# Two-layer encoder trunk: three PSUM accumulators for turned products and one for dense products, with pauses between dense blocks

## The chip, the core and the metric

The kernel runs on one core of a Trainium2 chip. The metric is the device time of one execution in microseconds. All computation is in float32 formats; products are made from pairs of a rounded part and its remainder.

## The reference

The input is a sequence of 2048 frames of width 1024. Layer 0 is a pooling mixer, layer 1 is attention; both end in a gated embedding add. Cut to what matters:

```python
# layer 0: h = rms_norm(x); u, z = split(h @ w_in); trailing means of u, group maps, * silu(z), @ w_out
# keys and values once from the stream after layer 0 (16 heads of 64)
def stick_breaking_attention(q, k, v):          # A[t,s] = beta[t,s] * prod_{s<j<t} (1 - beta[t,j])
    for blk in range(S // 128):
        logits = einsum('bhtd,bhsd->bhts', q_blk, k[:L]) * d ** -0.5
        log_keep = where(s < t, log_sigmoid(-logits), 0)
        later = cumsum(log_keep, reverse) - log_keep
        a = where(s < t, exp(log_sigmoid(logits) + later), 0)
        out = a @ v[:L]
# layer 1: x = x + (attention * silu(z)) @ b_w_out
# both layers: x = x + (p[i] @ ple_w[i]) * sigmoid(x @ ple_gate_w[i])
```

## The kernel before

The frames are cut into four chunks of 512. The first part (lines 144 to 547) runs layer 0, the keys and values and the queries for all chunks. It has PSUM pools of its own and is not touched.

The second part (from line 550) is attention with the rest of layer 1 beside it. PSUM has eight banks of 128x512 float32, and the pools divide them: `psl` (2) for logits, `psa` (2) for turned (transposed) products, `pso` (2) for a head's output, `psd` (2) for the dense products of the rest of the layer.

Chunks of queries are taken from the last (3) to the first (0). For each there are 16 heads, and for each head the chunks of keys from the queries' own down to 0: these are the slots. A slot has four steps `n`, one for 128 queries each. So chunk 3 has 256 steps, chunk 2 has 192, chunk 1 has 128 and chunk 0 has 64. The loop at line 808 issues in each step:

- `front` (lines 603 to 611): two matmuls into a `psl` tile (on the diagonal narrower ones and a third for the mask), a sigmoid on ScalarE into one of four `kap` tiles, and on VectorE a scan that makes running products into a `pp` tile.
- `turn` (lines 622 to 626), for the slot's step six steps back: up to four 128x128 transposes into a `psa` tile, a copy of it to `at[:, 0]` on ScalarE, and on VectorE the subtraction that makes the remainder `at[:, 1]`. The `psa` tile is free after both.
- some pieces of the `filler` (see below).
- `gather` (lines 634 and 635), for the step eight back: two matmuls of `at[:, 0]` and `at[:, 1]` with the values into the head's `pso` tile. After a head's last step ScalarE and VectorE take the output (lines 639 and 640), and after two heads GpSimd multiplies it by the gate (line 647).

The filler is a Python generator for dense work that has no part in the recurrence. Beside chunk 3 it is `gate_z`: the gate z for all four chunks, 32 blocks of 24 matmuls (lines 663, 665, 667), each read by VectorE (`zr`, line 704). Beside chunk 2 it is `post(3)`: the output projection, 8 blocks of 24 read by VectorE (`xr`, line 728); then for each of 8 column blocks the gate's 24 matmuls, read by ScalarE (`sg`, line 750), and 6 matmuls of the embedding, read by VectorE (line 753), and four transposes of the result into a `psa` tile (`psao`, line 760). The embedding itself is turned into `psa` tiles too (`psap`, line 737). Beside chunk 1 runs `post(2)`, beside chunk 0 `post(1)`. `post(0)` runs alone at the end, the tail, and takes three of four accumulators from `psl` and the fourth from `psd`.

`piecewise` yields after each matmul, and the loop draws as many pieces in a step as the rate says: pieces in all by steps of the chunk (`POSTZ / 64.0` is 3 a step, `POST / (64.0 * c3 - 2 * LAG_G)` is 2.5, 3.9 and 9.2). What it does not draw in a step is owed to the next.

The order in which the loop issues is a priority: a scheduler then places the instructions of each engine, with its own reckoning of when operands and buffers are there. Each engine runs its instructions in the placed order.

Of the kernel before, what the change touches and what calls it, by code (L numbers as in the profile page):

```python
# [8 lines left out]
F32 = mybir.dt.float32  # L9
# [5 lines left out]
P = 128  # L15
# [6 lines left out]
W5 = 512  # L22
# [8 lines left out]
def f(ap):  # L31
    return ap.bitcast(F32)
# [3 lines left out]
def trunk_kernel(ctx, tc, x, p, a_norm, a_w_in, a_w_group, a_scale, a_w_out, kv_norm, w_kv,  # L36
# [103 lines left out]
    def pair(nm):  # L140
        return act.tile([P, 2, W5], F32R, tag="act", name=nm)


    with ExitStack() as st:
# [4 lines left out]
        psd = st.enter_context(tc.tile_pool(name="psd", bufs=6, space=bass.MemoryType.PSUM))  # L149
        pst = st.enter_context(tc.tile_pool(name="pst", bufs=2, space=bass.MemoryType.PSUM))  # L150

        def dense():
            return psd.tile([P, W5], F32, tag="psd", name="psd")
# [396 lines left out]
    with ExitStack() as st:  # L550
# [1 line left out]
        t2 = st.enter_context(tc.tile_pool(name="s2", bufs=2))  # L552
        kap = st.enter_context(tc.tile_pool(name="kap", bufs=1))
        psl = st.enter_context(tc.tile_pool(name="psl", bufs=2, space=bass.MemoryType.PSUM))
        psa = st.enter_context(tc.tile_pool(name="psa", bufs=2, space=bass.MemoryType.PSUM))
        pso = st.enter_context(tc.tile_pool(name="pso", bufs=2, space=bass.MemoryType.PSUM))
        psd = st.enter_context(tc.tile_pool(name="psd2", bufs=2, space=bass.MemoryType.PSUM))

        NK = 4
        kaps = [kap.tile([P, W5], F32, name=f"kap{i}") for i in range(NK)]  # L560
# [89 lines left out]
        tail = [0]  # L650

        def dense():
            if tail[0] and tail[0] % 4:
                tail[0] += 1
                return psl.tile([P, W5], F32, tag="psl", name="psdt")
            if tail[0]:
                tail[0] += 1
            return psd.tile([P, W5], F32, tag="psd", name="psd")

        def piecewise(ps, units, acts, c0):  # L660
# [9 lines left out]
        def stored(src):  # L670
            units = []
            for u in [src[:, 0], src[:, 1]] if len(src.shape) == 5 else [src]:
                pr = wpair.tile([P, 2, u.shape[2], P], F32R, tag="wpair", name="wpair")
                nc.sync.dma_start(out=f(pr), in_=u)
                units.append(pr)
            return units

        def pair_up(c):

            if len(ogs[c]) < len(outs[c]):  # L680
                os = outs[c][len(ogs[c])]
                pr = pair("og")
                A.copy(out=pr[:, 0], in_=os)
                V.tensor_tensor(out=pr[:, 1], in0=os, in1=f(pr[:, 0]), op=ALU.subtract)
                ogs[c].append(pr)

        def gate_z(c):

            xs = chunk[c]["x2"] if c == NSUB - 1 else []
            for o in range(len(xs), KT):  # L690
                pr = pair("xz")
                nc.sync.dma_start(out=f(pr), in_=x2p[c][o])
                xs.append(pr)
            ps = psa.tile([P, 4, P], F32, tag="psa", name="psar")
            for j in range(4):
                T.transpose(ps[:, j, :], r2s[c][:, j : j + 1].to_broadcast([P, P]), ident)
            rb = t2.tile([P, W5], F32, tag="rb", name="rb", bufs=1)
            A.copy(out=rb, in_=ps.rearrange("q j t -> q (j t)"))
            for o in range(KT):
                wz = stored(wzd[o])  # L700
                ps = dense()
                yield from piecewise(ps, wz, xs, 0)
                zr = t2.tile([P, W5], F32, tag="tmp", name="zr", bufs=4)
                V.tensor_tensor(out=zr, in0=ps, in1=rb, op=ALU.mult)
                sg = t2.tile([P, W5], F32, tag="tmp", name="sgz", bufs=4)
                A.activation(out=sg, in_=zr, func=AF.Sigmoid)  # L706
                G.tensor_tensor(out=zr, in0=zr, in1=sg, op=ALU.mult)  # L707
                nc.sync.dma_start(out=zd[c][o], in_=zr)
                if c == 0:
                    pair_up(NSUB - 1)  # L710

        POSTZ = 8 * 24
        POST = 8 * 24 + 8 * 30 + 9

        def post(c):

            pin = t2.tile([P, 4, PLE], F32, tag="pin", name="pin", bufs=1)
            nc.sync.dma_start(out=pin, in_=p[1, 0, c * W5 : (c + 1) * W5, :].rearrange("(j q) n -> q j n", q=P))
            x3, og = [], ogs[c]
            while len(og) < 8:  # L720
                pair_up(c)
            for o in range(KT):
                wo = stored(wod[o])
                xr = t2.tile([P, W5], F32, tag="tmp", name="xr", bufs=4)
                nc.sync.dma_start(out=xr, in_=x2d[c][o])
                ps = dense()
                yield from piecewise(ps, wo, og, 0)
                V.tensor_tensor(out=xr, in0=ps, in1=xr, op=ALU.add)
                pr = pair("x3")
                A.copy(out=pr[:, 0], in_=xr)  # L730
                G.tensor_tensor(out=pr[:, 1], in0=xr, in1=f(pr[:, 0]), op=ALU.subtract)
                x3.append(pr)
            pt_ = []
            for k in range(2):
                pt = psa.tile([P, W5], F32, tag="psa", name="psap")
                for j in range(4):
                    T.transpose(pt[:, j * P : (j + 1) * P], pin[:, j, k * P : (k + 1) * P], ident)
                pr = t2.tile([P, 2, W5], F32R, tag="ple", name="ple")
                A.copy(out=pr[:, 0], in_=pt)
                V.tensor_tensor(out=pr[:, 1], in0=pt, in1=f(pr[:, 0]), op=ALU.subtract)  # L740
                pt_.append(pr)
            yield
            late = []
            for o in range(KT):
                wg = stored(wgd[o])
                wl = stored(wld[o])
                ps = dense()
                yield from piecewise(ps, wg, x3, 0)
                sg = t2.tile([P, W5], F32, tag="tmp", name="sg", bufs=4)
                A.activation(out=sg, in_=ps, func=AF.Sigmoid)  # L750
                pl = dense()
                yield from piecewise(pl, wl, pt_, 0)
                V.tensor_tensor(out=sg, in0=pl, in1=sg, op=ALU.mult)
                (V if tail[0] else G).tensor_tensor(out=sg, in0=sg, in1=f(x3[o][:, 1]), op=ALU.add)
                V.tensor_tensor(out=sg, in0=sg, in1=f(x3[o][:, 0]), op=ALU.add)

                def finish(o=o, sg=sg):
                    pt = psa.tile([P, 4, P], F32, tag="psa", name="psao")
                    for j in range(4):
                        T.transpose(pt[:, j, :], sg[:, j * P : (j + 1) * P], ident)  # L760
                    ot = t2.tile([P, 4, P], F32, tag="ot", name="ot", bufs=1)
                    A.copy(out=ot, in_=pt)  # L762
                    nc.sync.dma_start(
                        out=out[0, c * W5 : (c + 1) * W5, o * P : (o + 1) * P].rearrange("(t q) n -> q t n", q=P),
                        in_=ot)

                if late:
                    late.pop()()
                late.append(finish)
                if c:  # L770
                    pair_up(c - 1)
                yield
            late.pop()()
            yield

# [15 lines left out]
        active, filler, owed, head = {}, beside(NSUB - 1), 0.0, {}  # L791
        rate = POSTZ / 64.0
        LAG_T, LAG_G = 6, 8
# [14 lines left out]
        for n in range(4 * len(slots) + LAG_G):  # L808
            i, j = divmod(n, 4)
            if i < len(slots):  # L810
                c, h, kc = slots[i]
                if j == 0:
                    if i == 0:
                        begin(0)
                    if i + 1 < len(slots):
                        begin(i + 1)
                front(active[i], j)
            i2, j2 = divmod(n - LAG_T, 4)
            if 0 <= i2 < len(slots):
                turn(active[i2], j2)  # L820
            owed += rate
            while owed >= 1.0:
                next(filler, None)
                owed -= 1.0
            i3, j3 = divmod(n - LAG_G, 4)
            if 0 <= i3 < len(slots):
                gather(active[i3], j3)
                if j3 == 3:
                    st3 = active.pop(i3)
                    c3 = st3["c"]  # L830
                    if len(outs[c3]) == 8 and c3 not in done:
                        done.add(c3)
                        for _ in filler:
                            pass
                        if c3:
                            filler = beside(c3 - 1)
                            rate = POST / (64.0 * c3 - 2 * LAG_G)
                            owed = 0.0
# [31 lines left out]
```

## Time and profile before

| | us |
|---|---|
| median of 3 runs | 2885.43 (2884.45 to 2885.85) |
| profiled execution | 2880.44 |
| its span, first to last instruction | 2878.4 |
| start of attention | 1422.3 |
| start of the tail | 2777 |

The profile gives busy time of each engine, groups of instructions by line, and who waited for whom. PE is TensorE's matmul side and PEld its weight loads; a wait of PEld begins when the load could have begun, so it is longer than the same wait on PE. DVE is VectorE, ACT ScalarE, POOL GpSimd. Matmuls overlap in the trace: a row's length is from start to drained, and their pace is seen from the starts of neighbours. Some matmul records are missing. L626 is line 626 of the kernel before.

### The profile page before, as it was taken

Reading aid. Unit: us, or ns where it says so; the run is one execution under the profiler, and the core shown is the slowest. Engines: PE = TensorE matmul, PEld = TensorE weight load, DVE = VectorE, ACT = ScalarE, POOL = GpSimd, SP = SyncE. Lnnn points to the kernel's source line nnn. Section 1 sums busy time; section 2 is a strip of 40 time slices with the busy share of each in tenths; the row PEclk is TensorE's granted clock in tenths of the full one; section 3 lists DMA queues with packets and bytes.
Section 4 is the critical chain, followed back from the end, with each engine's and each line's share of the span. In section 5 each row is a group of like instructions: output and inputs, shape, how many; then the busy total and the mean of one; then the engine's idle time right before and its main releaser. Section 6 shows DMA issues by size and latency. Waiting matters only on the chain. (4 is left out here: it accounts for less than half of the span.)

```text
span 2878.4 us, 40091 instructions
## 1 busy us (share of the span) xinstructions
PE 2784.2 (97%) x13923; PEld 2297.6 (80%) x13923; DVE 1910.2 (66%) x2584; ACT 1407.0 (49%) x2765; POOL 856.8 (30%) x710
## 2 busy tenths in 40 slices
PE   8899999999999999999999999999999999999999
PEld 6688887888878888888777888787878778878877
DVE  6555534455455544455299999999999998886642
ACT  5444523345334542345355555556666665554431
POOL 3564346542574326643211111110100011111110
PEclk9899999999999999999999999999999999999999
DMA  7855697456954578346756565455555565567764
GB/s 271 279 185 200 208 299 236 142 191 220 317 199 164 196 229 299 103 153 209 219 182 222 164 213 168 157 164 178 165 158 164 161 189 183 186 189 250 233 205 159
DMA packets 335134, 576.39 MB, mean 200 GB/s; under 512 B 32783, under 2 KB 161839, under 8 KB 334933
## 3 DMA queue, kind: packets, MB, share of 16 engines
q1 hardware_dynamic: 329032, 565.39, 60.0%
q10 hardware_dynamic: 5900, 8.46, 1.0%
q8 instruction: 110, 1.80, 0.3%
q14 instruction: 92, 0.75, 0.1%
HBM read 433.16 MB, written 132.19 MB: 196 GB/s over the span
## 5 line engine op out<-in xcount | busy, mean ns | idle before, releaser
L362 PE MATMUL psd<-wpair,x 128*128 128x512 f32 x2304 | 543.9, 393 | 0.0
L609 ACT ACTIVATE kap<-psl 128x512 f32<-128x512 f32 (+3 forms) x640 | 341.8, 534 | 410.7 <-PE psl L604 258.8
L611 DVE TENSOR_TENSOR_SCAN pp<-kap,pp,zeros 128x512 f32<-128x512 f32 x384 | 513.7, 1339 | 30.0 <-ACT kap L609 28.2
L362 PEld LDWEIGHTS psd<-wpair,x 128*128 128x128 f32 x2304 | 428.1, 188 | 86.2
L626 DVE TENSOR_TENSOR at<-psa,at 128x512 fp32r<-128x512 f32 (+3 forms) x640 | 373.8, 585 | 16.7 <-ACT at L625 15.7
L622 PE MATMUL psa<-ident,pp 128*128 128x128 f32 x2176 | 350.6, 276 | 32.8 <-DVE at L626 30.1
L625 ACT CAST at<-psa 128x512 fp32r<-128x512 f32 (+3 forms) x640 | 331.3, 518 | 38.4 <-PE psa L622 34.5
L622 PEld LDWEIGHTS psa<-ident,pp 128*128 128x128 f32 x2176 | 251.4, 141 | 111.6 <-DVE at L626 68.3
L611 DVE TENSOR_TENSOR_SCAN pp<-kap,zeros 128x128 f32<-128x128 f32 (+3 forms) x256 | 228.8, 895 | 69.6 <-ACT kap L609 67.8
L603 PE MATMUL psl<-kk,qa 128*128 128x512 f32 (+3 forms) x640 | 234.3, 366 | 5.8 <-ACT vr L399 5.8
L634 PE MATMUL pso<-at,vv 128*128 128x512 f32 (+3 forms) x640 | 235.2, 368 | 0.7 <-ACT at L625 0.6
L604 PE MATMUL psl<-kk,qb 128*128 128x512 f32 (+3 forms) x640 | 234.3, 366 | 0.0
L635 PE MATMUL pso<-at,vv 128*128 128x512 f32 (+3 forms) x640 | 233.4, 365 | 0.0
L133 PE MATMUL psd<-xp,wpair 128*128 128x512 f32 x512 | 200.9, 393 | 7.9 <-ACT wpair L116 5.4
L117 DVE SCALAR_TENSOR_TENSOR wpair<-wraw,gains,wpair 128x512 fp32r<-128x512 f32 x192 | 149.9, 787 | 87.7 <-ACT wpair L116 87.4
L116 ACT ACTIVATE wpair<-wraw,gains 128x512 fp32r<-128x512 f32 x192 | 137.4, 720 | 137.5 <-DMA wraw<-in_w_kv_dram 85.6
L135 PE MATMUL psd<-xp,wpair 128*128 128x512 f32 x512 | 200.0, 391 | 2.6 <-DVE wpair L117 2.6
L134 PE MATMUL psd<-xp,wpair 128*128 128x512 f32 x512 | 200.2, 391 | 0.0
L707 POOL TENSOR_TENSOR zr<-zr,sgz 128x512 f32<-128x512 f32 x32 | 62.9, 1964 | 444.6 <-ACT sgz L706 296.2
L112 POOL TENSOR_TENSOR wpair<-wraw,wpair 128x512 fp32r<-128x512 f32 x107 | 145.7, 1366 | 80.3 <-ACT wpair L110 57.4
L110 ACT CAST wpair<-wraw 128x512 fp32r<-128x512 f32 x160 | 96.7, 618 | 121.8 <-PE psd L135 71.0
L603 PEld LDWEIGHTS psl<-kk,qa 128*128 128x128 f32 x640 | 120.7, 189 | 26.5 <-ACT vr L399 6.2
(209 smaller groups left out, 5594.1 us busy)
## 6 DMA issues: line engine op xcount, KB each, us to landing
wpair<-wi SPq DMA_DIRECT2D x96, 512.0 KB
kk<-kd SPq DMA_DIRECT2D x320, 128.0 KB
vv<-vd SPq DMA_DIRECT2D x160, 256.0 KB
wraw<-in_w_kv_dram SPq DMA_DIRECT2D x128, 256.0 KB
wpair<-wzd SPq DMA_DIRECT2D x64, 512.0 KB
wpair<-wod SPq DMA_DIRECT2D x64, 512.0 KB
wpair<-wgd SPq DMA_DIRECT2D x64, 512.0 KB
wi<-wpair SPq DMA_DIRECT2D x32, 512.0 KB
```

The source lines that it names most:

```text
L133: T.matmul(ps, wst(units, kt, 0, c0), acts[kt][:, 0], start=(kt == order[0]), stop=False)
L134: T.matmul(ps, wst(units, kt, 0, c0), acts[kt][:, 1], start=False, stop=False)
L362: T.matmul(pss2[i], ck["x2"][kt][:, xh, tk], wst(ws, kt, wh, 0, W5), start=(kt == 0 and xh == 0 and wh == 0), stop=(kt == KT - 1 and wh == 1))
L603: T.matmul(ps[:, :w], qa[:, qs], kk[:, :w], start=True, stop=False)
L604: T.matmul(ps[:, :w], qb[:, qs], kk[:, :w], start=False, stop=not st["diag"])
L609: A.activation(out=kp[:, r0:], in_=ps[:, :w], func=AF.Sigmoid, scale=-1.0)
L611: V.tensor_tensor_scan(out=pp[:, r0:][:, ::-1], data0=kp[:, r0:][:, ::-1], data1=zeros.to_broadcast([P, w]), initial=1.0 if st["diag"] els ...
L622: T.transpose(pt[:, j * P : (j + 1) * P], pp[:, r0 + kt * P : r0 + (kt + 1) * P], ident)
L625: A.copy(out=at[:, 0, cs], in_=pt[:, cs])
L626: V.tensor_tensor(out=at[:, 1, cs], in0=pt[:, cs], in1=f(at[:, 0, cs]), op=ALU.subtract)
L634: T.matmul(po[:, cs], vv[:, kt, :], at[:, 0, cs], start=(st["diag"] and kt == 0), stop=False)
L635: T.matmul(po[:, cs], vv[:, kt, :], at[:, 1, cs], start=False, stop=(st["last"] and kt == 3))
```

## The change

`psa` gets a third bank and `psd` keeps one. The filler now yields a marker, `PAUSE`, after each dense block, and the loop stops drawing pieces for the rest of the step when it meets one; what is owed stays owed. In the embedding add there is one between the gate's block and the embedding's as well. The rates count the markers (3.1 a step in chunk 3, 2.6, 4.1 and 9.5 after). In the tail the accumulators come in turn from `psl`, `pso` and, one in five, `psd`.

In the placed order of the changed program nothing differs before attention. At its start 24 dense matmuls stand ahead of the third front instead of 36. In chunk 3 the dense matmuls keep their places but for one block end of each head, where the two gather matmuls go ahead of the next block. In chunks 2 to 0 the next block begins a `front`, a `turn` and a `gather` after the end of the one before, where it often followed at once; the steps that lose their dense matmuls so are followed by fuller ones. A dozen of the readers move ahead of a scan on VectorE, some move behind one. No instruction is added.

```diff
-        psa = st.enter_context(tc.tile_pool(name="psa", bufs=2, space=bass.MemoryType.PSUM))
+        psa = st.enter_context(tc.tile_pool(name="psa", bufs=3, space=bass.MemoryType.PSUM))
...
-        psd = st.enter_context(tc.tile_pool(name="psd2", bufs=2, space=bass.MemoryType.PSUM))
+        psd = st.enter_context(tc.tile_pool(name="psd2", bufs=1, space=bass.MemoryType.PSUM))
...
         def dense():
-            if tail[0] and tail[0] % 4:
-                tail[0] += 1
-                return psl.tile([P, W5], F32, tag="psl", name="psdt")
+
             if tail[0]:
                 tail[0] += 1
+                if tail[0] % 5:
+                    pool, tag = ((psl, "psl"), (pso, "pso"))[tail[0] % 2]
+                    return pool.tile([P, W5], F32, tag=tag, name="psdt")
             return psd.tile([P, W5], F32, tag="psd", name="psd")
...
                 if c == 0:
                     pair_up(NSUB - 1)
-
-        POSTZ = 8 * 24
-        POST = 8 * 24 + 8 * 30 + 9
+                yield PAUSE
+
+        PAUSE = "the one accumulator is being read"
+        POSTZ = 8 * 25
+        POST = 8 * 25 + 8 * 32 + 2
...
                 x3.append(pr)
+                yield PAUSE
...
                 A.activation(out=sg, in_=ps, func=AF.Sigmoid)
+                yield PAUSE
                 pl = dense()
...
                 if c:
                     pair_up(c - 1)
-                yield
+                yield PAUSE
...
             owed += rate
             while owed >= 1.0:
-                next(filler, None)
                 owed -= 1.0
+                if next(filler, None) == PAUSE:
+                    break
```

## The prediction

> **What bounds the kernel now.** I read the page's busy shares first, then the attention part cut into stretches, one for each chunk of queries (3, 2, 1, 0) and the tail, and then who TensorE waits for in each.
>
> ```profile
> PE 2784.2 (97%) x13923; PEld 2297.6 (80%) x13923; DVE 1910.2 (66%) x2584; ACT 1407.0 (49%) x2765; POOL 856.8 (30%) x710
> ...
> 1422.30:1949.10 526.80, 509.29 (x2769) 420.71 (x2770) 474.00 (x561) 297.32 (x594) 78.58 (x40) 0.99 0.58 184
> 1949.10:2315.20 366.10, 352.27 (x1982) 289.86 (x1980) 344.74 (x432) 227.66 (x467) 36.29 (x25) 1.00 0.54 166
> 2315.20:2585.20 270.00, 262.26 (x1484) 219.58 (x1482) 236.68 (x308) 156.60 (x340) 33.44 (x24) 1.00 0.60 186
> 2585.20:2777.00 191.80, 184.43 (x1031) 156.45 (x1030) 121.63 (x191) 94.16 (x225) 32.20 (x25) 1.00 0.71 227
> 2777.00:2878.40 101.40, 95.09 (x439) 78.48 (x437) 23.52 (x34) 15.43 (x26) 10.31 (x8) 0.98 0.56 182
> ```
>
> The columns behind the length are PE, weight loads, VectorE, ScalarE, GpSimd, clock and DMA. TensorE is busy 96 to 97% of each attention stretch, but VectorE is close behind in the first two: 474.00 of 526.80 (90%) and 344.74 of 366.10 (94%). In the third it is 88% and in the fourth 63%. So chunk 3 is TensorE's by a little, chunk 2 belongs to both, chunks 1 and 0 are TensorE's. The clock was 0.99 or 1.00, so it has no part in this. Nothing ahead of 1422 us is touched.
>
> What TensorE waits for in attention is one thing, the accumulator of turned products. The rows give time in all, number, longest; there is one for each of the four chunk stretches, in order, from the weight loads (which stop first when PE stalls), and then the same wait on the matmul side over the whole run:
>
> ```profile
> PEld psa L622 <- DVE at L626: 28.2, 44, 2.0
> PEld psa L622 <- DVE at L626: 24.6, 41, 1.9
> PEld psa L622 <- DVE at L626: 10.1, 20, 0.9
> PEld psa L622 <- DVE at L626: 5.4, 10, 1.1
> ...
> PE psa L622 <- DVE at L626: 30.1, 51, 1.6
> ```
>
> So the change has between 30.1 us (matmul side) and 68.3 us (the four rows added) to win here. The dense accumulator has no such row: with two of them nothing ever waited for its reader. All that the single one costs is therefore new, and has to be worked out from how late the readers are.
>
> **The change, part by part.** *Third accumulator for turned products.* The transposes of a step no longer wait for the subtraction (L626) of two steps before, but of three. Not all of the lead is usable: the gather of the same step (L635) needs the subtraction of two steps before as well, and stands behind the four transposes and three dense matmuls. So a wait is not removed but put off by 0.41 us of transposes (1773.30 to 1773.71 below) and 3 x 0.23 of dense work (starts of neighbouring dense matmuls further down: 1433.53, 1433.76), 1.1 us. One head of chunk 3 shows what that is worth, around its last step:
>
> ```profile
> 1767.30 0.40 PE L667 MATMUL psd<-xz,wpair 128*128 128x512 f32 x1
> ...
> 1768.60 0.48 PE L663 MATMUL psd<-xz,wpair 128*128 128x512 f32 x1
> ...
> 1768.99 0.68 DVE L704 TENSOR_TENSOR zr<-psd,rb 128x512 f32<-128x512 f32 x1
> ...
> 1770.41 1.30 POOL L707 TENSOR_TENSOR zr<-zr,sgz 128x512 f32<-128x512 f32 x1 [14.71 <-DVE os L640]
> 1770.43 2.36 DVE L611 TENSOR_TENSOR_SCAN pp<-kap,pp,zeros 128x512 f32<-128x512 f32 x1
> ...
> 1771.68 0.40 PE L604 MATMUL psl<-kk,qb 128*128 128x512 f32 x1
> ...
> 1772.82 0.42 DVE L626 TENSOR_TENSOR at<-psa,at 128x256 fp32r<-128x256 f32 x1
> ...
> 1773.30 0.42 PEld L622 LDWEIGHTS psa<-ident,pp 128*128 128x128 f32 x4 [1.65 <-DVE at L626]
> 1773.30 0.66 PE L622 MATMUL psa<-ident,pp 128*128 128x128 f32 x4 [1.22 <-DVE at L626]
> ...
> 1773.71 0.48 PE L663 MATMUL psd<-xz,wpair 128*128 128x512 f32 x1
> ```
>
> VectorE has the reader of the dense block (zr, 0.68), the head's output and a scan that took 2.36 us while GpSimd worked beside it; so the subtraction ends at 1773.24, and PE goes from L604 at 1771.68 to L622 at 1773.30, 1.62 us where 0.23 is normal: 1.39 us lost. With three accumulators these transposes need an older subtraction, long done, and the gather that needs this one comes 1.1 us later, when it has ended. So 1.39 us a head go. Chunk 3 has 16 heads, the first without a predecessor: 15 x 1.39 = 20.9 us, of the 28.2 in the row (a load's wait overstates: 1.65 for these 1.39, so 0.84 of it counts).
>
> *One accumulator for dense products.* The first matmul of a block now waits until the reader of the block before is done. I take the end of the reader in the trace, 0.06 us for the signal (in the rows above, 1773.24 to 1773.30), and the PE work that the changed program puts between the two blocks. In chunk 3 a head has two block ends. At the one quoted, the last matmul starts at 1767.30 and zr ends at 1769.67; the changed program's order keeps the next step's front and two transposes between them and moves that step's two gather matmuls ahead of the new block, which would start at 1768.60 + 2 x 0.23 = 1769.06 and can't before 1769.73: stall 0.67 us. With the two transposes at half of the 0.41 that four take (some records of them are missing here) it is 0.6, which I take. The other end falls in the middle of the head:
>
> ```profile
> 1783.41 0.60 ACT L609 ACTIVATE kap<-psl 128x512 f32<-128x512 f32 x1 [0.97 <-PE psl L604]
> ...
> 1784.05 1.28 DVE L611 TENSOR_TENSOR_SCAN pp<-kap,pp,zeros 128x512 f32<-128x512 f32 x1
> 1784.12 0.39 PE L667 MATMUL psd<-xz,wpair 128*128 128x512 f32 x1
> ...
> 1785.47 0.47 PE L663 MATMUL psd<-xz,wpair 128*128 128x512 f32 x1
> ...
> 1785.83 0.68 DVE L704 TENSOR_TENSOR zr<-psd,rb 128x512 f32<-128x512 f32 x1
> ```
>
> Here the order stays as it was. zr ends at 1786.51, and the new block, which started at 1785.47, can't before 1786.57: 1.10 us, with no wait near it that could give it back. In the order of chunk 3 the pause thus moves little: its blocks already end with a step. Sum: 13 middles x 1.10, three with four more transposes between at 0.7, and 15 head ends x 0.6 = 14.3 + 2.1 + 9.0 = +25.4 us.
>
> The Trainium skill (Perfetto Trace Analysis, section Matmuls) says that independent groups of matmuls should rotate through different PSUM banks, so that the evacuation of one lies beside the matmuls of the next. The rows above agree that it lies there now. Taken strictly it would charge the single bank with the reader's whole lag less one matmul, 2.2 us for each of these 31 ends or +68 us, against my +25 with the attention work between as cover.
>
> *Start of attention.* With two accumulators PE runs 36 dense matmuls ahead while ScalarE still drains the stage before; with one it has 24.
>
> ```profile
> 1433.53 0.39 PE L667 MATMUL psd<-x,wpair 128*128 128x512 f32 x1
> 1433.76 0.39 PE L663 MATMUL psd<-x,wpair 128*128 128x512 f32 x1
> ...
> 1435.77 0.28 ACT L609 ACTIVATE kap<-psl 128x128 f32<-128x128 f32 x1 [4.84 <-DMA vd<-vv]
> ...
> 1436.47 0.33 PE L603 MATMUL psl<-kk,qa 128*128 128x384 f32 x1
> ```
>
> The third front needs the first one's accumulator, free at 1436.05. So PE stands from 1433.76 until then, some 2.3 us, and does the 12 matmuls (2.7 us) later: +2.5. Chunk 3: -20.9 + 25.4 + 2.5 = **+7.0 us**.
>
> *Chunk 2.* Here the pauses do put work between the blocks, where before many followed each other at once: a step passes without dense matmuls, and the next gets five or six. With the readers as late as they are, 9 of the 23 ends fall short, by 3.7 us together. The gain is bounded not by TensorE's 24.6 but by what VectorE has to give:
>
> ```profile
> DVE pp L611 <- ACT kap L609: 12.3, 28, 0.8
> DVE sg L755 <- POOL sg L754: 6.7, 7, 1.1
> ```
>
> Of its 366.10 - 344.74 = 21.4 us idle, 12.3 are starvation by late fronts, which an earlier PE can end; the 6.7 for GpSimd stay. Between -12.3 and nothing I take **-9 us**, nearer the first, since PE's own waits are twice as much.
>
> *Chunks 1 and 0.* TensorE alone. The waits were 10.1 and 5.4 us on the load side; the transposes of the embedding share the pool:
>
> ```profile
> PEld psap L737 <- DVE at L626: 2.0, 2, 1.6
> PEld psap L737 <- DVE at L626: 1.6, 1, 1.6
> ```
>
> That makes 12.1 and 7.0, and with the 0.84 from above a gain of 10.2 and 5.9. Against that stands one end of each:
>
> ```profile
> 2450.79 0.40 PE L667 MATMUL psd<-ple,wpair 128*128 128x512 f32 x1
> ...
> 2451.83 0.48 PE L663 MATMUL psd<-x,wpair 128*128 128x512 f32 x1
> 2451.86 0.67 DVE L753 TENSOR_TENSOR sg<-psd,sg 128x512 f32<-128x512 f32 x1
> ...
> 2620.72 0.39 PE L667 MATMUL psd<-og,wpair 128*128 128x512 f32 x1
> ...
> 2621.18 0.68 DVE L728 TENSOR_TENSOR xr<-psd,xr 128x512 f32<-128x512 f32 x1
> ```
>
> At the first the order between stays as it is, the reader ends at 2452.53 and 0.76 us are lost. At the second the pause puts 0.52 us of PE work between, the start is due at 2620.72 + 0.23 + 0.52 = 2621.47 and the reader is done at 2621.92: 0.45. Over all ends that fall short (15 of 23 in each chunk) this adds up to 8 and 9.5 us. Net **-2.2 and +3.6 us**.
>
> *Tail.* Blocks go round five accumulators of three pools. The last stretch had 95.09 us of PE in 101.40 with two pools, and every one of the five comes back only after three blocks or more; I cost it at nothing, hidden by that distance; a short turn would cost about a reader's 0.7 us each. The order of DMA issues on SP moves by a few places; weights come a block ahead, and in the group of all these matmuls one wait of 1.2 us is all there is, at the first block, so nothing there either:
>
> ```profile
> L663 PE MATMUL psd<-x,wpair 128*128 128x512 f32 x256 | 111.3, 435 | 1.2 <-DMA wpair<-wzd 1.2
> ```
>
> The pauses themselves add no instruction.
>
> **The sum.** +7 - 9 - 2.2 + 3.6 = -0.6 us on an execution of 2880.44 us (span 2878.4 and 2.0 around it). The runs have a median of 2885.43, 5.0 above, so I forecast 2885 us (2884.8).
>
> **Rivals.** (1) *The lead wins.* VectorE's lag is the real trouble: where PE stalls for the reader, VectorE catches up, and later waits that I kept vanish too. For it: chunk 2 has hardly any stall, and the readers can go ahead of a scan where the pause lets them. Then chunk 3 is 0 (its 20.9 become 28.2), chunk 2 -12, chunks 1 and 0, with half of their stalls absorbed, -6 and -1: -19, 2866 us.
>
> (2) *The single bank decides, slower.* With three turned accumulators PE runs further ahead of VectorE, and the reader, which stands in VectorE's order behind a scan (1.28 us or, beside GpSimd, 2.36) and a subtraction, comes later by that lead. The place is the dense block's first matmul (L663), the price up to the usable 1.1 us more at each of the 54 ends of chunks 3 and 2. It decides as soon as the reader's lag passes the 1.3 to 2.3 us of work between, which in chunk 3 it does already. Half of the ends at 1.1 is +30, with my -0.6 +29: 2914 us. Against it: in chunk 3 VectorE had caught up by the middle of the head (the scan at 1784.05 began as ScalarE's 1783.41 ended), so the lead is gone there. The Trainium skill's rule on rotating banks (Perfetto Trace Analysis, section Matmuls) speaks for this rival.
>
> (3) *Nothing much happens,* because the scheduler places instructions by its own reckoning and undoes the pauses; the order in chunk 3 hardly differs. That would be my sum without chunk 2's gain: +8, 2894 us.
>
> **How the numbers follow.** A measurement can tell this kernel from itself by about 0.2%, 5.8 us. I give my forecast 0.45, of which the spread of the terms (chunk 3 by 5, chunk 2 by 4, the others by 3 each, 8 together) puts 0.12 over 0.2% faster and 0.09 over 0.2% slower; rival 1 has 0.22, rival 2 0.23 and rival 3 0.10, 0.07 of it beyond 5.8. So faster 0.34, same 0.27, slower 0.39. The range, 2866 to 2906, leaves out the outer half of rival 1 and a third of rival 2.
>
> **What would show it.** Right: the load-side wait of L622 for L626 falls below 15 us in all; a new wait of the dense first matmul (L663 of before) for zr, of 20 to 30 us over chunk 3 at about 1.1 us a middle; chunk 3 longer by some 7 us, chunk 2 shorter by 5 to 12 with VectorE over 95% busy, PE idle for 2 to 3 us ahead of the third front. Wrong: the wait of L622 stays above 30 us or comes back at L634 and L635, chunk 2 gets longer, or the stall at L663 in chunk 3 is under 0.3 or over 2 us each.

## The result, and the profile after

The changed kernel takes 2905.26 us (median of 5, 2903.49 to 2908.51) against 2885.30 (median of 5, 2883.93 to 2885.85): a ratio of 1.0067, 95% interval 1.0054 to 1.0079. It is slower by 20 us where no change was forecast. The time lies at the upper edge of the stated range (2866 to 2906), which reached that far for the sake of rival 2 and not of the sum. Its profiled execution took 2905.26 us, with a span of 2903.3.

The engines' busy time, from the page of the changed kernel:

```profile
PE 2794.6 (96%) x13923; PEld 2309.4 (80%) x13923; DVE 1905.0 (66%) x2584; ACT 1401.9 (48%) x2765; POOL 842.2 (29%) x710
```

Its four attention chunks, 3 to 0, by stretches, in the columns that the prediction used:

```profile
1426.20:1972.50 546.30, 515.85 (x2769) 426.15 (x2770) 474.54 (x561) 298.29 (x594) 64.17 (x40) 0.98 0.55 178
1972.50:2335.00 362.50, 351.98 (x1986) 293.68 (x1984) 344.94 (x434) 224.71 (x468) 34.40 (x25) 1.00 0.54 168
2335.00:2607.70 272.70, 263.01 (x1487) 220.76 (x1486) 233.38 (x306) 155.38 (x340) 33.73 (x24) 1.00 0.59 186
2607.70:2795.20 187.50, 179.95 (x999) 152.38 (x997) 118.50 (x189) 90.16 (x218) 31.39 (x24) 1.00 0.72 227
```

Chunk 3 went from 526.8 to 546.3 us, chunk 2 from 366.1 to 362.5, chunk 1 from 270.0 to 272.7. Chunk 0 went from 185.7 to 187.5 and the tail from 107.5 to 108.2, both cut at the tail's first instruction (the prediction's last two rows are cut 6 us later; their sum is the same). That is +21.1 us in attention and the tail. Attention began 3.9 us later in this execution, but the program ahead of it is the same and the runs below begin it anywhere from 1423.8 to 1429.6, so that part is no effect. VectorE's work in chunk 3 is unchanged (474.00 and 474.54). TensorE's instructions are as many as before (2769), but it stands 13 us longer (526.80 less 509.29 before, 546.30 less 515.85 now), and the other 6.6 us are longer rows of its own. The granted clock has a part in those: behind its first 9 us it was 1.00 throughout chunk 3 before, and in the changed kernel it was 0.50 for 3.4 us each from 1441.1, 1871.2 and 1939.5, each time beside a wait of TensorE (2.93, 2.06 and 2.06 us). At half the clock these three stretches can cost 5 us at most, which is an estimate (half of 10.2). The prediction's word that the clock has no part held for the kernel before alone.

What TensorE stands for shows first in the groups of the changed kernel's page (busy, mean ns, idle before and what ended it), for the transposes and the gathers over the whole run:

```profile
L622 PE MATMUL psa<-ident,pp 128*128 128x128 f32 x2176 | 347.8, 275 | 1.2 <-DVE at L626 1.1
...
L635 PE MATMUL pso<-at,vv 128*128 128x512 f32 (+3 forms) x640 | 236.0, 369 | 7.7 <-DVE at L626 7.1
```

Then its waits (us in all, times, longest): three rows of chunk 3, two of chunk 2 and one each of chunks 1 and 0. (L664 is the dense block's first matmul, L705 its reader in chunk 3; L663 and L704 before.)

```profile
DVE pp L611 <- ACT kap L609: 44.1, 120, 1.7
PEld psd L664 <- DVE zr L705: 35.0, 30, 2.3
PE psd L664 <- DVE zr L705: 24.9, 30, 2.1
...
PEld pso L635 <- DVE at L626: 7.7, 16, 1.1
PEld psd L664 <- DVE xr L731: 4.8, 5, 1.3
...
PEld pso L635 <- DVE at L626: 4.2, 7, 1.0
...
PEld pso L635 <- DVE at L626: 3.3, 7, 0.9
```

The change did what it says: the transposes' wait fell from 30.1 us to 1.1 over the run. In its place stand the dense first matmul, most of all in chunk 3, and from chunk 2 on the gathers. VectorE now waits 44.1 us for fronts in chunk 3, where in the kernel before it was

```profile
DVE pp L611 <- ACT kap L609: 25.0, 78, 0.7
```

so it starves longer while TensorE, which feeds the fronts, waits for it.

Why the reader is late shows in the middle of a head, in the timeline of the changed kernel (start, us, engine, line):

```profile
1797.14 1.27 DVE L611 TENSOR_TENSOR_SCAN pp<-kap,pp,zeros 128x512 f32<-128x512 f32 x1
...
1798.33 0.39 PE L668 MATMUL psd<-xz,wpair 128*128 128x512 f32 x1
...
1798.34 0.66 DVE L626 TENSOR_TENSOR at<-psa,at 128x512 fp32r<-128x512 f32 x1
...
1798.92 1.27 DVE L611 TENSOR_TENSOR_SCAN pp<-kap,pp,zeros 128x512 f32<-128x512 f32 x1
...
1800.11 0.66 DVE L626 TENSOR_TENSOR at<-psa,at 128x512 fp32r<-128x512 f32 x1
...
1800.69 0.67 DVE L705 TENSOR_TENSOR zr<-psd,rb 128x512 f32<-128x512 f32 x1
...
1801.42 0.50 PE L664 MATMUL psd<-xz,wpair 128*128 128x512 f32 x1 [1.50 <-DVE zr L705]
```

VectorE runs without a break here. Behind the last matmul of the block (1798.33) it still has a subtraction, a scan and another subtraction before zr, which starts 2.36 us later and lets TensorE go on 3.09 us after that matmul. In the kernel before this lag was 1.71 us in nearly every middle of a head. Over chunk 3's 15 middles behind the first, the distance from the last matmul of a block to the first of the next is now 2.45 us in seven, 3.1 in five and 3.65 in three.

### The profile page after: what moved, and what is told of

The parts are those of the page before. It is cut to its first block, busy times and chain, and to the rows that moved or that the text cites. A ratio compares the mean times of both kernels' runs of the same rounds, so it can differ in the third digit from the quotient of the medians.

```text
span 2903.3 us, 40066 instructions
## 1 busy us (share of the span) xinstructions
PE 2794.6 (96%) x13923; PEld 2309.4 (80%) x13923; DVE 1905.0 (66%) x2584; ACT 1401.9 (48%) x2765; POOL 842.2 (29%) x710
## 5 line engine op out<-in xcount | busy, mean ns | idle before, releaser
L622 PEld LDWEIGHTS psa<-ident,pp 128*128 128x128 f32 x2176 | 259.3, 141 | 53.6 <-DVE at L626 2.3
L635 PE MATMUL pso<-at,vv 128*128 128x512 f32 (+3 forms) x640 | 236.0, 369 | 7.7 <-DVE at L626 7.1
L634 PE MATMUL pso<-at,vv 128*128 128x512 f32 (+3 forms) x640 | 240.6, 376 | 0.0
L708 POOL TENSOR_TENSOR zr<-zr,sgz 128x512 f32<-128x512 f32 x32 | 48.3, 1510 | 477.8 <-ACT sgz L707 290.1
L635 PEld LDWEIGHTS pso<-at,vv 128*128 128x128 f32 x640 | 120.8, 189 | 40.9 <-DVE at L626 17.6
```

Of the source, the lines that this page charges most:

```text
L622: T.transpose(pt[:, j * P : (j + 1) * P], pp[:, r0 + kt * P : r0 + (kt + 1) * P], ident)
L634: T.matmul(po[:, cs], vv[:, kt, :], at[:, 0, cs], start=(st["diag"] and kt == 0), stop=False)
L635: T.matmul(po[:, cs], vv[:, kt, :], at[:, 1, cs], start=False, stop=(st["last"] and kt == 3))
```

## The experiments

Theory A: the terms simply add, and the dense stalls are larger than worked out. Theory B: both waits are the same lag of VectorE, so a third turned accumulator only moves TensorE from one to the other while the dense reader stands in VectorE's queue. C: the pauses cost.

**The pauses alone.**

```diff
 (changed kernel)
-psa bufs=3 ... psd2 bufs=1
+psa bufs=2 ... psd2 bufs=2
```

> The changed kernel with two accumulators of each kind as before; only the pauses, their rates and the order of the tail are new. Theory A (what costs is that the one dense accumulator waits for its reader; the pauses by themselves are free): chunk 3 within 3 us of the 526.8 of before, no wait of the dense first matmul for zr, the wait for the turned products back at 25 to 30 us in chunk 3; in all 2885 within 4. Theory C (the pauses cost, since the dense matmuls that cover VectorE come in bursts): the loss of the changed kernel is here without its banks, 2895 to 2905, most of it in chunk 3.

2892.21 us, ratio 1.0016 (1.0007 to 1.0025). Chunk 3 of this run, as a stretch:

```profile
1429.60:1959.50 529.90, 509.58 (x2768) 420.65 (x2769) 473.96 (x561) 297.39 (x594) 78.67 (x40) 0.99 0.60 184
```

And its turned wait there:

```profile
PEld psa L622 <- DVE at L626: 28.1, 44, 2.0
```

0.0016 of 2887.24 is 4.6 us, a little more than A's 4 and far from C's 10 to 20. In chunk 3 the 529.9 hold a wait of 3.4 us for the first dense weights, which varies from run to run (1.2 before). In the waits of the kernel before, and then of this run, it reads:

```profile
PE psd L663 <- DMA wpair<-wzd: 1.2, 1, 1.2
```

```profile
PE psd L664 <- DMA wpair<-wzd: 3.4, 1, 3.4
```

All chunk 3 lengths in the table below are therefore given less this wait. The turned wait is as before, so C falls for chunk 3. Where the 4.6 us come from is not shown; they lie in chunks 2 and 1 in the main (367.7 and 271.8 us against 366.1 and 270.0), and chunks 2, 1 and 0 of this execution each hold a stretch of 3.4 us at a granted clock of 0.50, which the kernel before does not.

**The banks alone.**

```diff
 (kernel before)
-psa bufs=2 ... psd2 bufs=2
+psa bufs=3 ... psd2 bufs=1     (and the tail's five in turn)
```

> The kernel before with three accumulators for turned products and one for dense ones, without the pauses and at the old rates (the tail takes its five in turn). Theory A: chunk 3 as in the changed kernel, 543 to 550, since its blocks end with a step anyway; in chunks 2, 1 and 0 the blocks follow each other at once, so 23 ends each lose a reader's lag of 1 to 2 us less what two matmuls cover: 15 to 35 us a chunk, in all 2945 to 3000. Theory C: without the pauses the loss goes, 2885 to 2895.

2913.74 us, 1.0092 (1.0078 to 1.0105); chunk 3 546.2 us, as A said, but chunks 2 to 0 only 365.2, 273.8 and 191.7: some 3, 1 and 4 us above the changed kernel. I had that at 15 to 35 us a chunk, since I took the blocks to follow each other at once. In this trace at least four other TensorE instructions stand between two blocks at every end in chunks 2 to 0, where the kernel before often has none: with one accumulator the scheduler places them there itself. So with one dense accumulator the pauses save about 7 us (1.0092 against 1.0067), with two they cost 4.6, and in chunk 3 they change no more than 2 us (less the wait for weights, 543.0 without and 544.9 with them).

**One dense accumulator, two turned ones.**

```diff
 (changed kernel)
-psa bufs=3
+psa bufs=2
```

> The changed kernel with two accumulators for turned products in place of three (one dense accumulator, pauses and rates kept; one bank of eight is unused). Theory A, terms that simply add: the wait for zr in chunk 3 stays at 35 us, the turned waits of 20 us come back, chunk 3 is 564 to 568 and the whole 2935 to 2945. Theory B (the third accumulator's lead is what makes the reader late): the wait for zr falls to 22 to 27 us, the head middles all show a reader that starts 1.7 us behind the last matmul, chunk 3 is 552 to 558 and the whole 2915 to 2928.

2922.87 us, 1.0121 (1.0108 to 1.0135). Chunk 3 as a stretch, two of its waits, and the middle of a head in the timeline:

```profile
1426.70:1973.50 546.80, 516.10 (x2769) 421.94 (x2770) 475.35 (x561) 299.74 (x594) 63.88 (x40) 0.99 0.57 178
```

```profile
PEld psd L664 <- DVE zr L705: 26.8, 30, 1.2
...
PEld psa L622 <- DVE at L626: 15.5, 27, 1.7
```

```profile
1802.80 0.39 PE L668 MATMUL psd<-xz,wpair 128*128 128x512 f32 x1
...
1803.93 0.67 DVE L626 TENSOR_TENSOR at<-psa,at 128x512 fp32r<-128x512 f32 x1
...
1804.52 0.68 DVE L705 TENSOR_TENSOR zr<-psd,rb 128x512 f32<-128x512 f32 x1
...
1805.25 0.50 PE L664 MATMUL psd<-xz,wpair 128*128 128x512 f32 x1 [0.85 <-DVE zr L705]
```

This decides between A and B. Without the third accumulator the reader is 1.72 us behind again, here and in all middles but one (1.91), and the wait for zr is 26.8 and not 35.0: theory B's numbers. And chunk 3 is no longer than with the third (546.8 and 546.3): all that it takes away there, it gives back. B's length for chunk 3 (552 to 558) was still too high, and A's (564 to 568) more so, as the turned wait had come back only to 15.5 and not to 28.2: while TensorE stands for the reader, VectorE catches up.

**ScalarE reads the dense block.** If the lag is VectorE's queue, another reader should end it.

```diff
 (changed kernel, gate_z)
-V.tensor_tensor(out=zr, in0=ps, in1=rb, op=ALU.mult)
+A.copy(out=sg, in_=ps)
+V.tensor_tensor(out=zr, in0=sg, in1=rb, op=ALU.mult)
```

> The changed kernel, but in chunk 3 the dense block is copied out of its accumulator by ScalarE (32 copies of 128x512 more) and VectorE multiplies the copy. Theory A and B (the single accumulator pays for VectorE's queue ahead of the reader): the wait of the dense first matmul in chunk 3 falls from 35 to under 12 us, chunk 3 from 546 to 515 to 527, the whole to 2872 to 2885. Rival D (PE is held by VectorE's pace in any case; the wait moves): the waits turn up at the fronts (kap later by 0.6 us a block) or at the gathers, chunk 3 stays over 538, the whole over 2897.

2874.89 us, 0.9956 (0.9943 to 0.9968): faster than both kernels. The same three views of it:

```profile
1423.80:1939.20 515.40, 507.78 (x2768) 424.90 (x2769) 470.99 (x561) 309.02 (x626) 78.47 (x40) 0.99 0.61 188
```

```profile
PEld pso L635 <- DVE at L626: 6.2, 11, 2.3
```

```profile
1779.25 0.39 PE L668 MATMUL psd<-xz,wpair 128*128 128x512 f32 x1
...
1779.73 0.59 ACT L705 COPY sgz<-psd 128x512 f32<-128x512 f32 x1
...
1780.61 0.48 PE L664 MATMUL psd<-xz,wpair 128*128 128x512 f32 x1
```

The copy starts 0.48 us behind the last matmul, in every block behind the first no later than 0.49, and the accumulator is free before TensorE comes back (1780.32 against 1780.61). No row of TensorE waiting for the reader is left in chunk 3; VectorE's multiply is still there, but TensorE doesn't wait for it.

**The same with two turned accumulators, and in the kernel before.**

> The kernel in which ScalarE copies the dense block of chunk 3 out of its accumulator, with two accumulators for turned products in place of three (one dense accumulator and the pauses stay). Theory B (the third accumulator is worth its waits only where the dense reader isn't in VectorE's queue): chunk 3 goes from 515.4 to 526 to 536 us with 20 to 28 us of turned waits on the load side, and the other chunks lose as they did with two turned accumulators and VectorE's reader (+7, +4, +5), so 2900 to 2912 in all. Rival E (the whole gain of chunk 3 is the reader's, and the third accumulator does nothing there, as with VectorE's reader, where chunk 3 was 546.3 with three and 546.8 with two): chunk 3 stays within 3 us of 515.4, in all 2888 to 2894.

> The kernel before, two accumulators of each kind and no pauses, with ScalarE's copy of the dense block in chunk 3. Theory A: nothing waits for this reader in the kernel before, VectorE's multiply stays (0.68 us from the accumulator, about as long from the copy), so chunk 3 stays at 524 to 530 us and the whole within 4 us of 2885. Rival F (what the copy brings has nothing to do with the accumulators): chunk 3 falls by 8 to 12 us here too, to 2873 to 2878.

The first took 2906.58 us, 1.0070 (1.0056 to 1.0083), the second 2887.61, 1.0005 (0.9996 to 1.0014). Chunk 3 as a stretch and its turned wait, of the first:

```profile
1425.60:1954.20 528.60, 509.97 (x2768) 421.77 (x2769) 474.29 (x561) 313.16 (x626) 78.30 (x40) 0.99 0.59 184
```

```profile
PEld psa L622 <- DVE at L626: 26.2, 43, 2.0
```

And of the second:

```profile
1426.80:1953.40 526.60, 510.25 (x2769) 419.88 (x2769) 471.78 (x561) 313.58 (x626) 84.54 (x40) 0.99 0.60 185
```

```profile
PEld psa L622 <- DVE at L626: 26.8, 44, 2.0
```

The first is as theory B said, the second as theory A; rivals E and F fall. Chunk 3 in us, less the wait for the first weights (the first column is without the pauses, which change little there: 526.5 with them and VectorE's reader):

| dense reader in chunk 3 | 2 turned, 2 dense | 2 turned, 1 dense | 3 turned, 1 dense |
|---|---|---|---|
| VectorE | 525.6 (before) | 543.4 | 544.9 (changed) |
| ScalarE | 524.8 | 526.8 | 513.5 |

One dense accumulator costs 17.8 us with VectorE's reader and 2.0 with ScalarE's. The third turned one is worth -1.5 us in the first row and 13.3 in the second. Each length is from one execution, and the -1.5 can't be told from nothing: the same banks without pauses give 543.0, and the changed kernel's 544.9 holds two more stretches at half the clock than the 543.4 beside it.

**The start of attention.**

```diff
 (kernel with ScalarE's copy, gate_z)
+if c == NSUB - 1 and o == 0: ps = psa.tile(...)
+else: ps = dense()
```

> The kernel with ScalarE's copy in chunk 3 alone, and the very first dense block of attention placed in an accumulator for turned products, so that 36 dense matmuls stand ahead of the third front as before and not 24. Theory (the fill costs what the front's wait shows and the slow matmuls behind it): the wait of the third front for kap falls from 3.3 to under 1.5 us, the matmuls behind it start 0.23 us apart and not 0.43, chunk 3 is 4 to 6 us shorter, 2868 to 2871. Rival: the 12 matmuls are only moved, the wait comes back at the gathers of the first head, and chunk 3 stays within 1.5 us.

2875.30 us, 0.9957 (0.9944 to 0.9969), so no gain in the median. The waits of fronts and gathers in chunk 3, first without and then with the edit:

```profile
PE psl L603 <- ACT kap L609: 3.3, 1, 3.3
PE pso L635 <- DVE at L626: 2.5, 4, 1.8
```

```profile
PE psl L603 <- ACT kap L609: 1.3, 1, 1.3
PE pso L635 <- DVE at L626: 2.9, 4, 2.3
```

The third front's wait fell by 2.0 us, the longest of the gathers' rose by 0.5, and chunk 3 is 511.4 us by the table's measure, 2.1 less: between the two forecasts. Behind that front the matmuls are 0.23 to 0.35 us apart again; of the two stretches of slow ones that the kernel without the edit has there, one is left, beside a gather's wait of 2.26 us. The fill is worth some 2 us at most, and the runs do not settle it closer. In the changed kernel's timeline it looks like this:

```profile
1437.29 0.39 PE L668 MATMUL psd<-x,wpair 128*128 128x512 f32 x1
1440.61 0.44 PE L603 MATMUL psl<-kk,qa 128*128 128x384 f32 x1 [2.93 <-ACT kap L609]
...
1441.97 0.63 PE L604 MATMUL psl<-kk,qb 128*128 128x512 f32 x1
1442.39 0.31 PE L606 MATMUL psl<-maskr,identr 128*128 128x128 f32 x1
```

**ScalarE reads everywhere.** Chunks 2 to 0 had 5, 7 and 6 waits for xr, and some for the embedding's product.

```diff
 (changed kernel with ScalarE's copy, post)
+A.copy(out=xc, in_=ps)
-V.tensor_tensor(out=xr, in0=ps, in1=xr, op=ALU.add)
+V.tensor_tensor(out=xr, in0=xc, in1=xr, op=ALU.add)
+A.copy(out=lc, in_=pl)
-V.tensor_tensor(out=sg, in0=pl, in1=sg, op=ALU.mult)
+V.tensor_tensor(out=sg, in0=lc, in1=sg, op=ALU.mult)
```

> The changed kernel with ScalarE copying every dense block out of its accumulator that VectorE read (zr in chunk 3, xr and the product of the embedding in the others, 96 copies in all, 56 of them before the tail). Theory: the stalls of the dense first matmul in chunks 2, 1 and 0 (3.9, 7.1 and 4.9 us) fall to under 2 each, 10 to 14 us less than the kernel with zr alone, 2861 to 2866. Rival: chunk 2 has no room, VectorE is busy 95% there and its multiplies stay, and ScalarE's copies stand in front of the sigmoids; then chunk 2 stays within 2 us, the fronts' waits for kap grow, and the whole is 2868 to 2880.

2857.46 us, 0.9900 (0.9887 to 0.9914): the best version, 29 us below the kernel before. Its chunks 2, 1 and 0, as stretches:

```profile
1947.20:2303.30 356.10, 349.37 (x1986) 292.40 (x1984) 342.49 (x434) 232.56 (x485) 39.38 (x25) 1.00 0.57 171
2303.30:2568.00 264.70, 260.59 (x1485) 220.70 (x1485) 233.17 (x306) 162.98 (x356) 33.90 (x24) 1.00 0.66 193
2568.00:2752.20 184.20, 178.40 (x998) 152.17 (x997) 120.55 (x189) 99.13 (x234) 33.40 (x24) 1.00 0.74 225
```

They are 6, 8 and 3 us shorter than in the changed kernel. Against the version with zr alone that is 17 us, where I expected 10 to 14 (and 2861 to 2866 for the whole); VectorE is at 96% in chunk 2.

**The copies without the banks, and the banks without the pauses.**

> The kernel before, two accumulators of each kind and no pauses, with ScalarE's copies of zr, xr and the embedding's product. Theory (the copies matter only through the single accumulator; the third turned one then pays): nothing waits for these readers with two dense accumulators, so 2883 to 2891, and the 29 us that the changed kernel with the same copies stands below the kernel before belong to the two together. Rival F (the copies help by themselves, as they take PSUM reads off VectorE): 2870 to 2880.

> Three accumulators for turned products, one for dense ones and ScalarE's three kinds of copies, without the pauses and at the old rates. Theory (the pause buys the reader's lag, and with ScalarE that is 0.48 us and a copy of 0.59, 0.85 us behind the last matmul's own 0.23): blocks that follow each other at once lose up to 0.85 us at some 10 ends a chunk of chunks 2, 1 and 0, 5 to 15 us over the 2857.5 with pauses, 2862 to 2872. Rival (the pauses cost by themselves, as they did with two of each, 4.6 us, and the short reader needs none): 2850 to 2856.

The first took 2885.80 us, 0.9995 (0.9986 to 1.0004): the copies alone do nothing. The second took 2868.41, 0.9935 (0.9921 to 0.9948), 11 us over the one with pauses, inside its forecast, though the blocks do not follow each other at once here either: at least four TensorE instructions stand between them. So the 1% needs the accumulators as changed, the readers outside VectorE's queue and the pauses together; without the pauses 0.65% is left, without the copies the kernel is slower than before.

## Why the prediction was wrong

The step that failed is the term -20.9 in the sum of chunk 3 (-20.9 + 25.4 + 2.5 = +7.0, measured +19.5): the gain of the third turned accumulator, set beside the stalls of the single dense one as if the two were independent. The runs showed no net gain for it there. To see the terms, I add up for each pair of neighbouring TensorE instructions the distance between their starts beyond the normal one (0.23 us behind a 512-column matmul, less for narrower ones, 0.11 for a transpose), by what the later one is.

- *Stalls of the single accumulator, +25.4.* Right in size. With it and the pauses alone (two turned accumulators), this excess at dense first matmuls grew by 25.8 us, of which 2.2 are the longer wait for the first weights, so 23.6. At twelve of the 15 middles the next block then starts 2.45 us behind the last matmul where it was 1.36: 1.09 each, for the 1.10 of the prediction.
- *The turned waits, -20.9.* Wrong: the runs show -10.6 of it as a by-product of the stalls (the excess at the transposes fell from 22.3 to 11.7 with two turned accumulators), and nothing net for the third one. It took 9.6 us more from the transposes and 1.8 from the other turned products, but the dense first matmul got 8.0 us (the wait for weights taken out), the gathers 2.3, the rest 2.6. I had counted each wait as if the other stayed as it was. Both are one lag of VectorE, seen by TensorE at two places.
- *How the -20.9 was made.* The 1.39 us was read at one head end and taken for all 15. In the trace before it stands at seven, every second one (1.39 at 1512.5, 1578.3, 1642.7, 1773.3, 1840.3 and 1905.4, 1.74 at 1708.8): those where a scan took 2.36 us beside GpSimd. That the whole excess of 22.3 comes out near 20.9 is luck. The wait on the matmul side in chunk 3 of the kernel before gives less, and is nearer to the 13.3 us that the third accumulator is worth where ScalarE reads and nothing couples the two:

```profile
PE psa L622 <- DVE at L626: 13.6, 15, 1.6
```

- *The argument against rival 2.* "VectorE had caught up by the middle of the head" was read from a trace in which TensorE had just been held back for 1.39 us at the turned wait. With that wait gone the catching up went as well, in 8 of 15 middles. They are the very ones that the trace before shows behind such a wait: seven behind the seven head ends just named and one behind two shorter waits (0.50 at 1809.0, 0.70 at 1811.8). Of the seven middles whose lag stayed at 1.71, six had no turned wait of over 0.2 us between the middle before and themselves; only the first, at the start of attention, had. Rival 2 named this mechanism and its place; its price was too high for chunk 3 (8 us of the 30 that it had for two chunks).
- *Fill, +2.5.* A wait of 2.93 us was there, and a stretch at half the clock beside it that the prediction did not have; what they are worth in the end stays open between nothing and some 2 us.
- *Chunk 2, -9.* Measured -3.6. The stalls were as forecast (one accumulator and pauses cost 3.6: 366.1 to 369.7 with two turned ones, forecast 3.7), but the third turned one brought 7.2, where the net -9 needed nearly all of its bound of 12.3: VectorE's wait for fronts fell only to 8.5 us, and the gathers wait 7.7 where no such row stood.
- *Chunks 1 and 0, -2.2 and +3.6.* Measured +2.7 and +1.8. One accumulator and pauses cost 7.1 and 7.1 (forecast 8 and 9.5); the third turned one brought 4.4 and 5.3 (forecast 10.2 and 5.9). The 1.1 us by which the wait is put off did not cover it: it came back at L635, which the prediction had named as a sign of error.
- *Tail, 0.* 107.5 to 108.2; right. Rival 3 falls: the scheduler kept enough of the pauses that they save 7 us. Rival 1 saw that VectorE catches up during stalls, but not that this eats the gain.

The Trainium skill (Perfetto Trace Analysis, section Matmuls) wants independent groups of matmuls rotated through PSUM banks, so that one's evacuation lies beside the next one's matmuls. The runs agree in direction with VectorE's reader (17.8 us in chunk 3 for giving that up, not the 68 of the strict reading) and hardly at all with ScalarE's (2.0): what decides is whether the evacuation fits into the other work between two groups.

## What to carry to other kernels

Before giving a bank from one pool to another, look whose queue frees each: here one engine, VectorE, freed both, the waits were one lag, and more lead at one place came back as a later reader at the other. A single accumulator was nearly free (2.0 us in chunk 3) once its reader stood on an engine that got to it at once and the kernel had other matmuls to put between. Waits that end at the same engine must not be added up from a trace in which each hides part of the other; run one without the other. And before a stall is multiplied, count in the trace how often it occurs.

## What the runs showed of the hardware that was not expected

- A copy of a 128x512 accumulator by ScalarE started 0.43 to 0.49 us behind the start of the block's last matmul, at each of the 30 block ends behind the first, though ScalarE is busy 60% there (309.02 of 515.40 us); VectorE's read in the kernel before never started earlier than 1.69.
- Beside the 2.93 us of standing at the start of attention, the granted clock of the changed kernel was 0.50 for 3.4 us, and TensorE's matmuls came 0.42 us apart (1441.97 to 1442.39) where 0.23 is normal. The Trainium skill (TensorE: Matmul & The Clock Gate, Part 1) gives about 3.4 us as the window that decides on the slower clock; here stands shorter than that were enough, though not each of them. In the twelve traces, from 14 us into attention on, TensorE has 35 waits of 1.8 us or more, and 22 of them have such a stretch beside them.
- The wait for the first dense weights of attention was 1.2 to 4.0 us in executions of nearly the same program, so lengths of chunk 3 can't be compared to better than 3 us without taking it out.
